# A two-layer encoder trunk: splits moved to VectorE, two more early column blocks, modulation moved to other stages

## The chip, the cores and the metric

The kernel runs on one core of a Trainium2 chip, as one launch. The metric is the device time of a launch in microseconds; a profiled execution gives the trace. The engines are TensorE (PE; its weight loads are listed apart as PEld), VectorE (DVE), ScalarE (ACT), GpSimd (POOL) and SyncE (SP), whose queue issues nearly all DMAs. Each engine works through its own list of instructions in order and waits on semaphores.

## The reference, cut to what matters

x is 1024 tokens by 1024 channels. Each of two layers does the following:

```python
mod = silu(c) @ w_mod[l] + b_mod[l]            # six rows of 1024: sh_a sc_a gt_a sh_f sc_f gt_f
h = rms_norm(x, g_attn[l]) * (1 + sc_a) + sh_a
qa, ka, va, qb, kb, vb, qc, kc, vc = split_cols(h @ w_in[l], IN_SPLITS)
...                                            # three head groups A, B, C and their norms
x = x + gt_a * (y @ w_o[l])                    # output projection
h = rms_norm(x, g_ffn[l]) * (1 + sc_f) + sh_f
gate, up = split_cols(h @ w_gu[l], (2816, 2816))
x = x + gt_f * ((silu(gate) * up) @ w_down[l])
```

A final RMS norm closes the trunk. All is float32.

## The kernel before, in words

**Splits.** A matmul operand of full precision is held as two tiles: the high part, rounded by ScalarE (`act.copy`), and the low part, the rest, from a subtraction on a second engine. Three matmuls (`mm3`, line 190) make one product. `split_tile` (148) does this for a 128x1024 weight tile `wst` into `whi` and `wlo`; the subtraction is on GpSimd unless `eng` says otherwise. `split_to` (198) does it for 128x512 tiles. Weight tiles share the tag `whl` with eight buffers, the raw tiles the tag `wst` with two.

**Order in a layer.** Projection of group C, then V (8 blocks, 830) and the remaining A/B columns (12 half blocks, 981 to 992), then attention, the output projection (1475 to 1620), gate/up (1622 to 1829) and down. On engines that `pin` names, the order is that of the program; elsewhere it may be changed when the program is built.

**Output projection.** The 1024 tokens are worked off in two halves. In the first, `o_rows` (1500) takes a row block of w_o for six column blocks at once and two further columns follow (1532, 1548); in the second, a loop over eight columns (1596) follows. `w_next` (1481) keeps up to four split weight tiles ahead: row blocks 7, 0 and 1 are split by VectorE, the eleven others by GpSimd. `residual` (1494) adds the result to x, `square_sum` (400) sums the squares of x over channels into `ssq`, and `rstd_rows` (463) yields twice: after the statistics (`rstd_cols`, tile `ps_st`) and after the spread over partitions (`spread`, tile `ps_r`). `h_norm` and `h_shift_split` make the first token half's blocks h11 and h21 here.

**Gate/up.** It multiplies 2x2 blocks by seven products (`PRODUCTS`, 206): operands of h are 11, 21, t2, t1, t3, 22, t4. Column block q runs over 22 values, gate and up in turn. `gu_product` (1662) runs one product of four k, 12 matmuls, and drains it. Products 11, t2, t3 and t4 of a block accumulate in one PSUM bank "a", products t1 and 22 in "c", product 21 in "b". PSUM has eight banks (tag `mm`, bufs=8). Products 11 and 21 need only the first token half of h and single columns of weights, so those of the first EARLY=5 column blocks run first (1788 to 1803), on weights from `first_cols` (1745), while the second half of h is still made: `t2_part`, `t3_part` and `t4_part` (1755 to 1781) norm x, form sums and split them; four of each. The other five products of those blocks follow in the main loop (1808), where `a_parts` (221) forms and splits the weight sums, alternating VectorE and GpSimd by `turn`. `Ahead.fill(n)` makes them up to n ahead.

**Modulation.** Ten groups of 1024 columns (`todo`, 310) are still open when layer 0 starts. One step multiplies 128 rows of w_mod by their element of silu(c) and adds into the tile `acc` (VectorE, with a load of 512 KB); after eight steps a finish sums over partitions with four matmuls (`ps_mod`) and VectorE work. `mod_next` (350) does at most one step per call and finishes on the next; it is called in the V loop (977), once per half block of A/B (987), and in layer 0 in the output projection (1505, 1598). `mod_stream` (364) does the same in halves of 512 columns inside layer 0's gate/up (1783, called at 1822 from q=2 on).

Of the kernel before, what the change touches and what calls it, by code (L numbers as in the profile page):

```python
# [10 lines left out]
F32 = mybir.dt.float32  # L11
# [8 lines left out]
P = 128  # L20
D = 1024
S = 1024
KC = D // P
H = 512
FF = 2816
# [60 lines left out]
def trunk(ctx: ExitStack, tc, A, C, out):  # L86
# [90 lines left out]
    C_COLS = [(1408, 1920)]  # L177
    V_COLS = [(512, 768), (1280, 1408), (1920, 2048)]

    def w_cols(w, c0):  # L180

        return split_w(
            lambda v: [(v, w[:, c0 : c0 + P].rearrange("(k p) n -> p k n", p=P))], KC
        )

    def w_rows(w, r0, hl=None, eng=None):
# [34 lines left out]
    def a_parts(raws, sums, m, first, turn):  # L221

        def part(src):
            t = wp.tile([P, 2, 4, P], F32R, name="wpt", tag="whl", bufs=8)
            dst = t[:, 0, :m], t[:, 1, :m]
            turn[0] += 1
            split_to(dst, src, (dve, pool)[turn[0] % 2])
            return dst  # L230

        r1, r2 = raws
        a11, a21 = r1[:, :m, :P], r1[:, :m, P:]
        a12, a22 = r2[:, :m, :P], r2[:, :m, P:]
# [12 lines left out]
        yield part(a22)  # L247
# [63 lines left out]
    going = {"step": 0}  # L311

    def mod_parts(c, shared):
        pl, tag, bufs, width = shared
        acc = going["acc"]
        hi = pl.tile([P, width], F32R, name="acch", tag=tag, bufs=bufs)
        lo = pl.tile([P, width], F32R, name="accl", tag=tag, bufs=bufs)
        dve.tensor_copy(hi, acc[:, c])
        dve.tensor_tensor(out=lo, in0=acc[:, c], in1=f32(hi), op=ALU.subtract)
        going["parts"] = c.start, hi, lo, shared  # L320
        going["wait"] = width < 1024

    def mod_flush(psp):

# [22 lines left out]
        mod_finish(*todo.pop(0), sums)  # L347
        going["step"] = 0

    def mod_next(psp, shared, l):  # L350


        if psp is not None:
            mod_flush(psp)
        if not todo or todo[0][0] > l or going["step"] == KC:
            return
        if going["step"] == 0:
            going["acc"] = cp.tile([P, 1024], F32, name="acc", tag="acc")
        mod_step(*todo[0], going["step"], going["acc"], shared)
        going["step"] += 1  # L360
        if going["step"] == KC:
            mod_parts(slice(0, shared[3]), shared)
# [329 lines left out]
    for l in range(2):  # L692
# [281 lines left out]
        for t in range(8):  # L974
            v_split(t, early[t] if t < len(early) else v_proj(t))
            if t > 1:
                mod_next(psl, (ab, "zt", 4, 1024), l)

        wab = split_tile(wst.pop(0), KC)
        store = None  # L980
        for oc in range(NE, 8):
            w = wab
            for half in range(2):
                if half == 0 and oc < 7:
                    wab = split_tile(wst.pop(0), KC)
                ps = ab_proj(w, half)
                mod_next(psl, (ab, "zt", 4, 1024), l)
                if store:
                    store()
                if half == 0 and oc < 6:  # L990
                    wst.append(w_ab(l, oc + 2))
                store = ab_split(oc, half, ps, ab)
# [488 lines left out]
        def w_next():  # L1481

            while due and len(wq) < 4:
                kind, i = due.pop(0)
                eng = dve if kind == "row" and i in (7, 0, 1) else pool
                if kind == "row":
                    wq.append(w_rows(w_o, i * P, eng=eng))
                else:
                    wq.append(w_cols(w_o, i * P))
            return wq.pop(0)  # L1490

        pss = [psl.tile([P, 512], F32, name="ps_o", tag="mm") for _ in range(NK)]
# [7 lines left out]
        def o_rows(ki, hi, lo):  # L1500
            wh, wl = w_next()
            for n in range(NK):
                ns = slice(n * P, (n + 1) * P)
                mm3(pss[n], wh[:, ns], wl[:, ns], hi, lo, ki == 0, ki == 7)
            for _ in range(0 if l else (1, 1, 1, 1, 1, 0, 0, 0)[ki]):
                mod_next(None, (mp, "wm", 2, 1024), 0)

        for ki in range(5):
            o_rows(ki, yq[:, ki, 0:H], yq[:, ki, H:S])
# [85 lines left out]
        ssq = square_sum(ntp, xt, 0, 1)  # L1595
        for i, n in enumerate((6, 7, 0, 1, 2, 3, 4, 5)):
            w = wc[i] if i < KC - NK else w_next()
            if l == 0:
                mod_next(psl, (mp, "wm", 2, 1024), 0)
            if i < 4:  # L1600
                spill(0, range(2 * i, 2 * i + 2))
            ps = psl.tile([P, 512], F32, name="ps_o", tag="mm")
# [8 lines left out]
            if i == 3:  # L1611
                rows = next(norm)
                for k in range(KC):
                    h_norm(k, 0, rows)
                    h_shift_split(("11", "21")[k % 2], k // 2, xt[:, k, 0:H], shift(k))
        mod_flush(psl)
        ssq = square_sum(ntp, xt, 1, 1)
        spill(1)
        close(mp_cm)
# [4 lines left out]
        ff_cm, ffp = open_pool("ffn", side="left")  # L1624
        hb_cm, hbp = open_pool("hb", side="right")
        h_tiles(hbp, ("t2", "t1", "t4", "22", "t3"))
        turn = [0]

        def x_tile(n, shape, name):
            return xp.tile(shape, F32, name=name, tag=f"x{n}")  # L1630
# [31 lines left out]
        def gu_product(q, p, a):  # L1662
# [5 lines left out]
            lo, hi = slice(0, H), slice(H, S)  # L1668

            def take(key, out=None):  # L1670
                if out is None:
                    tag, bufs = ("u4", 1) if (q, num) == (4, 1) else ("u", 4)
                    out = ffp.tile([P, H], F32, name="u", tag=tag, bufs=bufs)
                t[key] = out
                act.copy(out, ps)
# [68 lines left out]

        def first_cols(c0):
            rows = w_gu[:, c0 : c0 + P].rearrange("(k h p) n -> h p k n", h=2, p=P)
            return split_w(lambda v: [(v[:, 4 * i : 4 * i + 4], rows[i]) for i in range(2)], KC)

        dsh = ffp.tile([P, 4], F32, name="dsh")
        for i in range(4):  # L1750
            sub(dsh[:, i : i + 1], shift(2 * i + 1), shift(2 * i))
        EARLY = 5
        early = [first_cols(q % 2 * FF + q // 2 * 2 * P) for q in range(4)]

        def t2_part(i, rows):

# [9 lines left out]
            sub(b11, b12, b11)  # L1766
            shifted_sub(t2, b22, shift(k + 1), b11)
            h_split("t2", i, t2, dve)
            h_split("t1", i, b11, pool)
            return b12, b21, b22, t2  # L1770

        def t3_part(i, b12, b21, b22, t2):

            shifted_sub(b12, b22, dsh[:, i : i + 1], b12)
            h_split("t3", i, b12, pool)

        def t4_part(i, b12, b21, b22, t2):

            h_shift_split("22", i, b22, shift(2 * i + 1))
            shifted_sub(b21, b21, shift(2 * i + 1), t2)  # L1780
            h_split("t4", i, b21, pool)

        mods_due = mod_stream(psl, (ntp, "sq", 2, H), (1, 4))
        bs = []
        rows = None
        norm = rstd_rows(ssq, ntp, psl)
# [1 line left out]
        for q in range(EARLY):  # L1788
            for i in range(2):
                a = [w[:, 4 * i : 4 * i + 4] for w in early[q]]  # L1790
                gu_product(q, PRODUCTS[i], a)
                if q == 0:
                    rows = next(norm)
            if q == 0:
                early.append(first_cols(2 * 2 * P))
                raw0 = gu_raw(0)
            if q < 4:
                bs.append(t2_part(q, rows))
            if q == 0:
                t3_part(0, *bs[0])  # L1800
                t4_part(0, *bs[0])
            if q == 3:
                ahead.fill(5)
        for part in (t3_part, t4_part):
            for q in range(1, 4):
# [2 lines left out]
        for q in range(NF):  # L1808
# [9 lines left out]
            for i, p in enumerate(PRODUCTS[2 if q < EARLY else 0 :]):  # L1818
                gu_product(q, p, ahead.get())
                ahead.fill()  # L1820
                g_step()
                if q > 1:
                    next(mods_due, None)
        for _ in mods_due:
            pass
# [313 lines left out]
```

## Time and profile before

| | |
|---|---|
| median of 3 runs | 2606.36 us |
| the runs | 2606.36, 2611.0, 2601.78 us |
| the profiled execution | 2610.04 us |
| its span, first to last instruction | 2608.3 us |
| mean granted TensorE clock | 0.975 |
| HBM read, written | 267.31 MB, 87.85 MB |

The profile lists for each engine its busy time, for groups of equal instructions (output tile <- input tiles) count, busy time and mean, and the idle time before them with the instruction that ended it (after "<-"). A window is a stretch of the span with the busy time of each engine; a timeline lists instructions in order with their start and duration. Nearly all instructions carry line 49, that of the helper which records them, so tiles are the way to find them. Durations of neighbouring instructions overlap a little.

### The profile page before, as it was taken

The page shows a single profiled execution, that of the slowest core. Times are in us where ns is not written, and L with a number is a line of the kernel's source. Part 1 is how long each engine was busy: PE and PEld are TensorE (multiplying, and loading weights), DVE is VectorE, ACT ScalarE, POOL GpSimd, SP SyncE. Part 2 cuts the span into 40 slices and gives each one's busy share as a digit, 9 for nine tenths or more (in the row PEclk, how much of TensorE's full clock was granted, in tenths as well). Part 3 has the DMA queues.
Part 4 walks back from the last instruction along what each step waited for, and adds up shares of the span by engine and source line. Part 5 has one row for each costly group of instructions (what it writes and reads, how often), then busy time and mean ns, then how long its engine had stood idle before and what let it go on. Part 6 is the DMA issues. An engine that isn't in the chain of part 4 may idle for free.

```text
span 2608.3 us, 34639 instructions
## 1 busy us (share of the span) xinstructions
PE 2455.3 (94%) x12071; PEld 2024.9 (78%) x12071; DVE 1836.1 (70%) x2916; ACT 1241.4 (48%) x2335; POOL 974.2 (37%) x881
## 2 busy tenths in 40 slices
PE   5899999988899999989998999998999999998998
PEld 4677899776677777878886779987877888886887
DVE  6845999987978786377657449998587455445865
ACT  5421888943433333334543128898444333333443
POOL 5641445643643444300044224465446434430001
PEclk9999999998999999999999999999999999998999
DMA  8467205165244543296432760151624233228643
GB/s 265 141 186 232 61 18 151 39 219 176 89 146 162 169 157 123 88 290 199 135 97 68 212 191 25 25 156 43 202 65 145 93 106 105 93 97 248 203 140 108
DMA packets 291166, 356.48 MB, mean 137 GB/s; under 512 B 33080, under 2 KB 207376, under 8 KB 290992
## 3 DMA queue, kind: packets, MB, share of 16 engines
q1 hardware_dynamic: 290688, 354.14, 44.1%
q8 instruction: 95, 1.56, 0.2%
q14 instruction: 79, 0.65, 0.1%
q0 software_dynamic: 304, 0.14, 0.0%
HBM read 267.31 MB, written 87.85 MB: 136 GB/s over the span
## 4 chain that ended last, share of the span: by engine, by line
PE 47%; DVE 7%; issue 4%; DMA 3%; ACT 2%; POOL 2%; SPq 1%; POOLq 0%; DVEq 0%; ACTq 0%
PE ps_w L49 19%; PE ps_d L49 12%; PE ps_o L49 3%; PE pv L49 3%; PE ps_ab L49 2%; PE T L49 2%; PE ps_v L49 2%; PE sC L49 2%; DMA wmt<-in_w_mod_dram 1%; SPq L49 1%; DVE wpt L49 1%; DVE acc L49 1%; DVE xb L49 1%; DVE sg L49 1%; DVE ws L49 1%
## 5 line engine op out<-in xcount | busy, mean ns | idle before, releaser
L49 PE MATMUL ps_d<-wpt 128*128 128x512 f32 x1848 | 432.1, 395 | 17.7 <-ACT wpt L49 17.3
L49 PEld LDWEIGHTS ps_d<-wpt 128*128 128x128 f32 x1848 | 350.1, 190 | 95.2 <-ACT wpt L49 18.4
L49 POOL TENSOR_SCALAR pr<-pr,rs 128x1024 f32<-128x1024 f32 (+4 forms) x256 | 208.1, 815 | 223.1 <-DVE rs L49 208.9
L49 POOL TENSOR_TENSOR wlo<-wst,whi 128x1024 fp32r<-128x1024 f32 x58 | 148.4, 2561 | 263.9 <-ACT whi L49 251.5
L49 PE MATMUL pv<-pt,vs 128*128 128x256 f32 x1216 | 200.7, 296 | 11.0 <-DVE y L49 4.9
L49 DVE TENSOR_TENSOR pt<-T,pt 128x512 fp32r<-128x512 f32 x304 | 199.7, 681 | 10.2 <-ACT pt L49 8.7
L49 PE MATMUL T<-identr,pr 128*128 128x128 f32 x1320 | 191.9, 274 | 5.5 <-POOL pr L49 2.6
L49 POOL TENSOR_TENSOR wpt<-ws,wpt 128x512 fp32r<-128x512 f32 x88 | 122.9, 1399 | 191.8 <-ACT wpt L49 136.1
L49 ACT CAST wpt<-w 128x512 fp32r<-128x512 f32 x154 | 95.6, 621 | 200.2 <-PE ps_d L49 184.8
L49 ACT CAST pt<-T 128x512 fp32r<-128x512 f32 x304 | 170.0, 586 | 40.3 <-PE T L49 38.4
L49 ACT COPY u<-ps_w 128x512 f32<-128x512 f32 x132 | 77.4, 586 | 219.4 <-PE ps_w L49 219.4
L49 POOL TENSOR_TENSOR sg<-sg,u 128x512 f32<-128x512 f32 x88 | 128.0, 1455 | 142.7 <-DVE u L49 70.8
L49 PEld LDWEIGHTS pv<-pt,vs 128*128 128x128 f32 x1216 | 160.6, 189 | 25.4 <-DVE y L49 12.5
L49 PEld LDWEIGHTS T<-identr,pr 128*128 128x128 f32 x1320 | 156.6, 141 | 27.5 <-POOL pr L49 4.7
L49 DVE TENSOR_TENSOR wpt<-w,wpt 128x512 fp32r<-128x512 f32 x154 | 108.0, 701 | 90.6 <-ACT wpt L49 90.6
L49 DVE SCALAR_TENSOR_TENSOR acc<-wmt,condT,acc 128x512 f32<-128x512 f32 (+1 forms) x99 | 125.1, 1273 | 46.9 <-DMA wmt<-in_w_mod_dram 46.4
L49 ACT CAST wpt<-ws 128x512 fp32r<-128x512 f32 x176 | 108.1, 622 | 70.8 <-PE ps_w L49 31.3
L49 DVE TENSOR_TENSOR wpt<-ws,wpt 128x512 fp32r<-128x512 f32 x88 | 83.5, 949 | 79.0 <-ACT wpt L49 78.9
L49 PE MATMUL ps_w<-ht3h,wpt 128*128 128x512 f32 x352 | 114.0, 406 | 15.0 <-ACT sg L49 15.0
L49 DVE TENSOR_TENSOR ws<-wr 128x512 f32<-128x512 f32 x88 | 87.4, 995 | 56.9 <-POOL wpt L49 53.4
L49 ACT CAST whi<-wst 128x1024 fp32r<-128x1024 f32 x74 | 77.2, 1049 | 104.2 <-PE ps_o L49 46.7
L49 DVE TENSOR_REDUCE rs<-sC 128x1 f32<-128x1024 f32 x96 | 116.9, 1220 | 10.2 <-PE sC L49 9.9
(258 smaller groups left out, 6279.4 us busy)
## 6 DMA issues: line engine op xcount, KB each, us to landing
wr<-in_w_gu_dram SPq DMA_DIRECT2D x92, 512.0 KB, 4.2
gpd<-sg SPq DMA_DIRECT2D x154, 256.0 KB, 4.5
graw<-gpd SPq DMA_DIRECT2D x76, 512.0 KB, 3.6
w<-in_w_down_dram SPq DMA_DIRECT2D x110, 256.0 KB, 5.3
wmt<-in_w_mod_dram SPq DMA_DIRECT2D x47, 512.0 KB, 5.2
qk<-qkd SPq DMA_DIRECT2D x44, 512.0 KB, 7.3
wmt<-in_w_mod_dram SPq DMA_DIRECT2D x66, 256.0 KB, 3.6
qkd<-qko SPq DMA_DIRECT2D x64, 256.0 KB, 3.8
```

What stands on the lines that cost most here:

```text
L49: ins = op(*args, **kwargs)
```

## The change

1. `w_cols` takes an engine, and `w_next` gives VectorE for all rows and columns of w_o. `first_cols` gives VectorE. `h_split` of t1, t3 and t4 goes to VectorE (t2 was there). `turn` starts at -10, which sends the first ten weight parts of gate/up to VectorE.
2. EARLY is 7. The weights of early block q+4 are fetched behind block q, and the raw tiles of the main loop after them. The statistics of the second half come behind both products of block 0, the spread behind block 1, the parts t2 of i behind block i+1, and five weight parts are made ahead behind block 5. The outputs of product 11 of blocks 5 and 6 lie in a tile that shares the buffer of `acc`.
3. No modulation step runs in the output projection. Beside V and A/B the calls are one per V block, as before, and two per A/B half block; they go up to group (0, 4) in layer 0 and through (1, 5) in layer 1. The stream in layer 0's gate/up starts at q=7 and takes (0, 5) to (1, 2). A finish always waits one call more.

```diff
-    def w_cols(w, c0):
+    def w_cols(w, c0, eng=None):
...
-            split_to(dst, src, (dve, pool)[turn[0] % 2])
+            split_to(dst, src, (dve, pool)[max(turn[0], 0) % 2])
...
-        going["wait"] = width < 1024
+        going["wait"] = True
...
-    def mod_next(psp, shared, l):
+    def mod_next(psp, shared, until):
...
-        if not todo or todo[0][0] > l or going["step"] == KC:
+        if not todo or todo[0] >= until or going["step"] == KC:
...
             if t > 1:
-                mod_next(psl, (ab, "zt", 4, 1024), l)
+                mod_next(psl, (ab, "zt", 4, 1024), ((0, 5), (2, 0))[l])
...
                 ps = ab_proj(w, half)
-                mod_next(psl, (ab, "zt", 4, 1024), l)
+                for _ in range(2):
+                    mod_next(psl, (ab, "zt", 4, 1024), ((0, 5), (2, 0))[l])
...
-                eng = dve if kind == "row" and i in (7, 0, 1) else pool
                 if kind == "row":
-                    wq.append(w_rows(w_o, i * P, eng=eng))
+                    wq.append(w_rows(w_o, i * P, eng=dve))
                 else:
-                    wq.append(w_cols(w_o, i * P))
+                    wq.append(w_cols(w_o, i * P, eng=dve))
...
-            for _ in range(0 if l else (1, 1, 1, 1, 1, 0, 0, 0)[ki]):
-                mod_next(None, (mp, "wm", 2, 1024), 0)
...
-            if l == 0:
-                mod_next(psl, (mp, "wm", 2, 1024), 0)
...
-        mod_flush(psl)
...
-        turn = [0]
+        turn = [-10]
...
             def take(key, out=None):
+                if num == 1 and 5 <= q < EARLY:
+                    out = spare[:, (q - 5) * H : (q - 4) * H]
...
-            return split_w(lambda v: [(v[:, 4 * i : 4 * i + 4], rows[i]) for i in range(2)], KC)
+            return split_w(
+                lambda v: [(v[:, 4 * i : 4 * i + 4], rows[i]) for i in range(2)], KC, eng=dve
+            )
...
-        EARLY = 5
+        EARLY = 7
         early = [first_cols(q % 2 * FF + q // 2 * 2 * P) for q in range(4)]
+        raw0 = None
+        spare = cp.tile([P, 1024], F32, name="spare", tag="acc")
...
-            h_split("t1", i, b11, pool)
+            h_split("t1", i, b11, dve)
...
-            h_split("t3", i, b12, pool)
+            h_split("t3", i, b12, dve)
...
-            h_split("t4", i, b21, pool)
+            h_split("t4", i, b21, dve)
...
-        mods_due = mod_stream(psl, (ntp, "sq", 2, H), (1, 4))
+        mods_due = mod_stream(psl, (ntp, "sq", 2, H), (1, 3))
...
                 gu_product(q, PRODUCTS[i], a)
-                if q == 0:
-                    rows = next(norm)
+            if q + 4 < EARLY:
+                early.append(first_cols((q + 4) % 2 * FF + (q + 4) // 2 * 2 * P))
+            elif raw0 is None:
+                raw0 = gu_raw(0)
             if q == 0:
-                early.append(first_cols(2 * 2 * P))
-                raw0 = gu_raw(0)
-            if q < 4:
-                bs.append(t2_part(q, rows))
-            if q == 0:
+                next(norm)
+            if q == 1:
+                rows = next(norm)
+            if 1 <= q < 5:
+                bs.append(t2_part(q - 1, rows))
+            if q == 1:
                 t3_part(0, *bs[0])
                 t4_part(0, *bs[0])
-            if q == 3:
+            if q == EARLY - 2:
                 ahead.fill(5)
...
-                if q > 1:
+                if q >= EARLY:
                     next(mods_due, None)
```

More of the change, by code (lines that the diff above doesn't have):

```diff
@@ L178, in trunk @@
     V_COLS = [(512, 768), (1280, 1408), (1920, 2048)]
-    def w_cols(w, c0):
+    def w_cols(w, c0, eng=None):
         return split_w(
-            lambda v: [(v, w[:, c0 : c0 + P].rearrange("(k p) n -> p k n", p=P))], KC
+            lambda v: [(v, w[:, c0 : c0 + P].rearrange("(k p) n -> p k n", p=P))], KC,
+            eng=eng,
         )
```

## The prediction, made before the changed kernel ran

> **What bounds the kernel now.** I read the page first, then the windows of equal stages in the two layers, then TensorE's timeline for the idle times inside them, and last VectorE's and GpSimd's lists at those places.
>
> ```profile
> span 2608.3 us, 34639 instructions
> PE 2455.3 (94%) x12071; PEld 2024.9 (78%) x12071; DVE 1836.1 (70%) x2916; ACT 1241.4 (48%) x2335; POOL 974.2 (37%) x881
> ...
> 1978.43 378.27 PE ps_w L49 x1620
> ```
>
> TensorE is the bound. In the chain of waits, gate/up of the second layer runs 1620 matmuls in 378.27 us without a break, 0.2335 us each. One early block (two products of 12 matmuls) is therefore 24 x 0.2335 = 5.6 us, and a product 2.8. A change can win only TensorE's idle time and the slow matmuls behind it. Both layers do the same work, but only the first carries modulation beside it, so windows of the same stage show where time goes (output projection; start of gate/up until the first t3 product; rest of gate/up; then the same for layer 1; columns: length, busy time and count of PE, PEld, DVE, ACT, POOL, granted clock, DMA share, GB/s):
>
> ```profile
> 528.50:629.70 101.20, 94.84 (x425) 77.57 (x424) 80.52 (x89) 39.43 (x52) 40.56 (x17) 0.98 0.69 226
> 629.70:688.20 58.50, 39.46 (x158) 30.86 (x156) 50.59 (x58) 26.06 (x42) 29.82 (x18) 0.84 0.19 59
> 688.20:1108.20 420.00, 408.26 (x1724) 326.26 (x1724) 301.70 (x357) 149.46 (x267) 183.52 (x125) 0.99 0.44 142
> 1817.00:1909.80 92.80, 92.80 (x421) 76.78 (x420) 60.97 (x73) 41.50 (x55) 41.48 (x18) 0.99 0.56 184
> 1909.80:1962.20 52.40, 40.33 (x157) 31.65 (x156) 44.62 (x51) 23.89 (x39) 27.43 (x17) 0.88 0.14 42
> 1962.20:2362.00 399.80, 399.71 (x1704) 321.15 (x1704) 206.23 (x245) 150.48 (x266) 171.97 (x125) 0.99 0.32 106
> ```
>
> The start of gate/up (rows two and five) holds 12 to 19 us of idle TensorE at a clock of 0.84 to 0.88; the output projection of layer 0 is 8.4 us longer than that of layer 1, and the rest of its gate/up 20.2 us longer. TensorE's own rows name the waits:
>
> ```profile
> 542.52 1.49 PE L49 MATMUL ps_r<-identr,rstd 128*128 128x128 f32 x8 [3.90 <-DVE rstd L49]
> 587.79 0.73 PE L49 MATMUL ps_mod<-acch,onesr 128*128 128x512 f32 x2 [1.48 <-DVE acch L49]
> 591.12 0.74 PE L49 MATMUL ps_mod<-accl,onesr 128*128 128x512 f32 x2 [0.98 <-DVE accl L49]
> 641.56 1.87 PE L49 MATMUL ps_st<-onesr,ssq 128*128 128x1 f32 x8 [8.67 <-DVE ssq L49]
> 688.26 1.22 PE L49 MATMUL ps_w<-ht3h,wpt 128*128 128x512 f32 x2 [8.09 <-ACT sg L49]
> ...
> 1915.59 1.87 PE L49 MATMUL ps_st<-onesr,ssq 128*128 128x1 f32 x8 [2.77 <-DVE ssq L49]
> 1946.87 0.50 PE L49 MATMUL ps_w<-ht2h,wpt 128*128 128x512 f32 x1 [1.64 <-ACT wpt L49]
> 1948.49 0.50 PE L49 MATMUL ps_w<-ht2h,wpt 128*128 128x512 f32 x1 [1.13 <-POOL wpt L49]
> 1950.09 1.05 PE L49 MATMUL ps_w<-ht2h,wpt 128*128 128x512 f32 x2
> 1962.22 1.22 PE L49 MATMUL ps_w<-ht3h,wpt 128*128 128x512 f32 x2 [6.55 <-ACT sg L49]
> ```
>
> All of them end at VectorE or at what follows it. At 1962.22 the releaser ACT is only the messenger: its copy of the product's bank stands in its queue behind a cast that waits for VectorE.
>
> ```profile
> 1961.06 0.62 ACT L49 CAST ht4h<-xb 128x512 fp32r<-128x512 f32 x1 [2.72 <-DVE xb L49]
> 1961.59 0.58 ACT L49 COPY sg<-ps_w 128x512 f32<-128x512 f32 x1
> ```
>
> Why VectorE is late shows when its rows are laid beside GpSimd's (first three lines VectorE, fourth GpSimd, then VectorE's groups from 1923 to 1964):
>
> ```profile
> 1930.06 0.68 DVE L49 TENSOR_TENSOR ht2l<-t,ht2h 128x512 fp32r<-128x512 f32 x1
> 1930.66 1.78 DVE L49 SCALAR_TENSOR_TENSOR xb<-xb,mod,t 128x512 f32<-128x512 f32 x1
> 1932.36 0.67 DVE L49 TENSOR_TENSOR u<-u,ps_w 128x512 f32<-128x512 f32 x1
> 1930.20 1.69 POOL L49 TENSOR_TENSOR ht3l<-xb,ht3h 128x512 fp32r<-128x512 f32 x1 [1.28 <-ACT ht3h L49]
> ...
> L49 DVE SCALAR_TENSOR_TENSOR xb<-xb,mod,t 128x512 f32<-128x512 f32 x4 | 6.0, 1508 | 0.0
> L49 DVE SCALAR_TENSOR_TENSOR h22l<-xb,mod,h22h 128x512 fp32r<-128x512 f32 x4 | 6.0, 1498 | 0.0
> L49 DVE SCALAR_TENSOR_TENSOR xb<-xb,gsc,ps_r 128x512 f32<-128x512 f32 x8 | 5.7, 736 | 0.0
> L49 DVE SCALAR_TENSOR_TENSOR xb<-xb,dsh 128x512 f32<-128x512 f32 x4 | 5.5, 1368 | 0.0
> L49 DVE TENSOR_TENSOR xb<-xb 128x512 f32<-128x512 f32 x4 | 5.2, 1298 | 0.0
> ```
>
> The VectorE operation that starts while GpSimd is in its split takes 1.78 us and ends 0.55 us after it; operations that read PSUM (the ps_r and ps_w rows) keep 0.74 and 0.67. Against 0.74 (0.68 for the plain subtraction) the four slow groups lose 4 x (0.77 + 0.76 + 0.63 + 0.62) = 11.1 us. With smaller excesses in groups not shown, I take 14 us of some 41.
>
> The Trainium skill, page "SBUF — State Buffer", section "SBUF: two separate sides", says that VectorE operations with two SBUF inputs and GpSimd operations exclude each other through one shared port pair for a whole instruction. These rows agree with it, including the untouched PSUM readers. By it the 14 us vanish with GpSimd's splits; if the slowness were VectorE's own, t3 would begin some 13 us later in each layer and the time would be 26 us above my sum.
>
> **The change part by part.** *Splits moved to VectorE (w_next, first_cols, h_split, first ten weight parts).*
>
> ```profile
> L49 POOL TENSOR_TENSOR wlo<-wst,whi 128x1024 fp32r<-128x1024 f32 x58 | 148.4, 2561 | 263.9 <-ACT whi L49 251.5
> ...
> 1818.80 1.23 DVE L49 TENSOR_TENSOR wlo<-wst,whi 128x1024 fp32r<-128x1024 f32 x1 [0.38 <-ACT whi L49]
> ```
>
> A 1024-wide split is 2.56 us on GpSimd and 1.23 on VectorE; a 512-wide one 0.68. Eleven splits per output projection cost VectorE 11 x 1.23 = 13.5 us; it is busy 61.0 of 92.8 us in layer 1 and, without the thirteen modulation steps, no more than that in layer 0, so they fit at no cost. Whatever queues behind such a split (residuals, ssq, h_norm) waits with it for its cast.
>
> The work on h's second half, as VectorE's busy time in a window, its last operation, and GpSimd's last split:
>
> ```profile
> 1923.10:1962.20 39.10, 39.10 (x42) 0.92 0.09 27
> 1962.62 1.77 DVE L49 SCALAR_TENSOR_TENSOR xb<-xb,mod,t 128x512 f32<-128x512 f32 x1
> 1965.49 1.74 POOL L49 TENSOR_TENSOR ht4l<-xb,ht4h 128x512 fp32r<-128x512 f32 x1
> ```
>
> From the first h_norm (1923.1) VectorE has no idle time until 1964.4, 41.3 us. Less 14, plus 12 splits of h (12 x 0.6, the distance of the 0.68 us rows above), two first_cols splits (2.5; the third falls earlier), three weight parts and two additions of early products (5 x 0.6): 41.3 - 14 + 7.2 + 2.5 + 3.0 = 40.0 us, with the low halves of h among it, whose last GpSimd now ends at 1967.2.
>
> *Seven early blocks.* The statistics move behind the second product, so ssq gets 2.8 us more cover: all of the 2.77 us wait of layer 1. In layer 0 the 8.67 us should go too, for its ssq additions stand behind modulation steps that are removed. The first h_norm then comes 5.6 + 1.9 (statistics) + 5.6 + 0.5 (spread) = 13.6 us after the start, against 13.3 now, but TensorE then still has five blocks (28 us) in place of four. The t3 product can begin 7 x 5.6 + 2.4 + 5.6 = 47.2 us after the start, or about 1957.1 on the old clock; VectorE has its last h at 1923.4 + 40.0 = 1963.4, and TensorE wants it, in the fourth k of t4, at 1964.8. That is tight. Remaining waits per layer: nothing at the low end, today's 6.55 + 1.64 + 1.13 = 9.3 us at the high end; I take 3.0, near the low end, because the work balances. So 50.2 us in place of 52.4. The rest of gate/up loses two blocks (11.2) and, with a shorter stall, about 1 us of slow matmuls (at 1950.09 two last 1.05 us): 399.8 - 12.2 = 387.6. **Layer 1: 452.2 - 437.8 = 14.4 us won.** The additional loads are two columns of 512 KB while DMA is at 42 GB/s: hidden.
>
> The Trainium skill, page "TensorE: Matmul & The Clock Gate", Part 1, puts the return to half rate after an idle window of about 3.4 us. Here the matmuls were already slow behind waits of 1.64 and 1.13 us; by the rule my 3.0 us would leave no slow matmuls and the sum would be 2 us lower in all.
>
> *Modulation out of layer 0's output projection.* Thirteen steps and their 512 KB loads leave VectorE and the SP queue, with one finish. The three waits at 542, 588 and 591 are 6.4 us, plus slow matmuls; layer 1 shows the stage without them: 101.2 - 92.8 = **8.4 us won** (5 to 9). The gate/up stream has four groups in place of four and a rest that ends a fifth: of 20.2 us it keeps four fifths, 16.2. So layer 0's gate/up goes from 58.5 + 420.0 = 478.5 to 437.8 + 16.2 = 454.0: **24.5 us won**.
>
> *More modulation beside the V and A/B projections.* Six more steps in layer 0, eight in layer 1:
>
> ```profile
> 209.27 0.71 PE L49 MATMUL ps_mod<-acch,onesr 128*128 128x512 f32 x2 [1.28 <-DVE acch L49]
> 195.00:262.00 67.00, 65.72 (x283) 52.96 (x282) 35.25 (x40) 10.78 (x16) 12.61 (x4) 1.00 0.77 232
> 1450.00:1460.00 10.00, 10.00 (x45) 8.10 (x44) 1.38 (x2) 0.89 (x2) 4.74 (x10) 1.00 0.91 319
> ```
>
> VectorE has 30 us to spare for 8 x 1.3. DMA goes from 232 to (15.5 + 3.1 MB) / 67 us = 279 GB/s, below the 319 seen nearby. The mod loads stand in SP's queue ahead of the qko stores and the next w_ab load, and that load is two blocks (22 us) ahead. Each layer gains one finish: four matmuls (1 us) and up to 1.3 of waiting. I take 1.5 per layer, **3.0 us lost** (0 to 5). That a finish now waits one call more gives VectorE time and costs nothing.
>
> Sum: 14.4 + 8.4 + 24.5 - 3.0 = 44.3 us. The profiled execution took 2610.04 (its span 2608.3), 3.7 above the median of the runs; 2606.4 - 44.3 = **2562 us**.
>
> **The rivals.** *PSUM runs out.* Bank "a" of every early block stays open until its last product, so seven of eight banks are held when block seven runs, and each second product waits for VectorE's addition of the one before.
>
> ```profile
> 1944.33 0.68 DVE L49 TENSOR_TENSOR u<-u,ps_w 128x512 f32<-128x512 f32 x1
> 1953.56 0.67 DVE L49 TENSOR_TENSOR u<-u,ps_w 128x512 f32<-128x512 f32 x1
> ```
>
> The second of these is the fifth block's, which ended at 1946.87 - 1.64 = 1945.2: it is 8 us late, the one before, 5.6 us earlier, some 5. If that lateness stays, TensorE waits as much as today: 9.3 - 3.0 + 2 (slow matmuls) = 8.3 us per layer, 2562 + 17 = 2579. For it: VectorE's balance has no slack. Against: the lateness is about the 14 us that go.
>
> *The DMA queue becomes the bound in A/B.* At two loads per half block TensorE's 5.6 us meet 1.05 MB of modulation, 0.52 of stores and 0.26 of weights; at today's 232 GB/s that is 7.9 us, 2.3 too long in some six halves per layer before the buffers' wait thins it out: 28 us, 2590. Against: 319 GB/s was reached.
>
> *Slower: VectorE inherits GpSimd's waits.* GpSimd stood 251.5 us waiting for whi casts, 4.3 for each of 58 splits. If 18 splits per layer make VectorE stand 3 us each, and everything behind them is late by as much, that is 108 us against 44 won: 2670. It decides from 1.2 us per split on. Against: the casts are paced by TensorE, as are the residuals behind them, and the split that VectorE already has there waits 0.38 us.
>
> **How the numbers follow.** Forecast 0.58 (its own range 2551 to 2574, from the bounds above), PSUM 0.18, DMA 0.10, the last two together with no net change 0.04, slower 0.10. A measurement of this kernel tells about 0.3% (8 us) from no change. Faster 0.86, same 0.04, slower 0.10. The range takes in the forecast's low end, PSUM and DMA: 2547 to 2592.
>
> **What would show it.** Right: VectorE's xb rows all at 0.74 from the start of gate/up; no ssq wait; t3 beginning 47 to 51 us after the first ps_w in both layers; the output projection near 93 us in layer 0; A/B still without idle TensorE. Wrong: ps_w waiting for DVE u (banks), a wait for wlo in the A/B projection (DMA), wlo rows on VectorE with idle time of 1.2 us or more and ps_o waiting behind them.

## The result, and the profile after

The changed kernel takes 2571.97 us (median of 4 runs, 2568.89 to 2575.07) against 2604.11 for the kernel before (median of 4, 2601.78 to 2611.0): ratio 0.9872, 95% interval 0.9847 to 0.9897. It is 32 us faster; 44 were forecast. The profiled executions differ by 35.0 us of span. The page's head:

```profile
span 2573.3 us, 34615 instructions
PE 2447.9 (95%) x12071; PEld 2023.2 (79%) x12071; DVE 1835.1 (71%) x2979; ACT 1240.3 (48%) x2331; POOL 830.9 (32%) x811
```

TensorE has the same 12071 matmuls and is busy 7.4 us less (fewer matmuls at a low clock); the rest, 27.6 us, is idle time that is gone. GpSimd has 70 instructions and 143 us of work less. VectorE has 63 instructions more and is busy for no longer: its operations became shorter.

To see where the 35.0 us come from, the span is cut at the first matmul of each stage. This table is worked out from the starts of TensorE's instructions (us). The prediction's windows were cut by eye and differ from these stages by up to 2 us.

| stage | before | after | difference | forecast |
|---|---|---|---|---|
| V and A/B projections, layer 0 | 168.7 | 178.8 | +10.1 | +1.5 |
| output projection, layer 0 | 101.5 | 91.7 | -9.8 | -8.4 |
| gate/up, layer 0, up to the first t3 product | 58.3 | 49.0 | -9.3 | -8.3 |
| the rest of it | 421.5 | 399.6 | -21.9 | -16.2 |
| V and A/B projections, layer 1 | 169.0 | 178.4 | +9.4 | +1.5 |
| output projection, layer 1 | 93.0 | 92.7 | -0.3 | 0 |
| gate/up, layer 1, up to the first t3 product | 52.4 | 49.0 | -3.4 | -2.2 |
| the rest of it | 401.8 | 388.8 | -13.0 | -12.2 |
| all other stages | 1142.1 | 1145.3 | +3.2 | 0 |

The +3.2 of the last row lies mostly ahead of layer 0's projections (+2.1) and in group C of layer 1 (+1.7), where the change does nothing; the experiments' runs differ there among themselves by as much (91.6 to 94.6 us and 44.8 to 47.9). The three gains came, that of layer 0's gate/up bigger than forecast. One term is far off: the V and A/B stages lost 19.5 us, not 3.0. The same windows as in the prediction, with the A/B stages added (length; busy time and count of PE, PEld, DVE, ACT, POOL; granted clock, DMA share, GB/s), first of before, A/B only:

```profile
92.60:261.30 168.70, 161.66 (x723) 129.07 (x723) 95.12 (x124) 43.88 (x84) 67.23 (x51) 0.98 0.66 189
1357.00:1526.00 169.00, 159.99 (x713) 128.43 (x712) 95.13 (x125) 45.47 (x86) 64.28 (x52) 0.97 0.50 146
```

and of after:

```profile
94.70:273.50 178.80, 166.03 (x728) 131.67 (x728) 115.56 (x139) 43.79 (x84) 66.44 (x51) 0.95 0.67 197
542.10:633.90 91.80, 91.80 (x423) 76.08 (x422) 64.17 (x88) 41.54 (x55) 6.58 (x4) 1.00 0.56 186
633.90:682.90 49.00, 46.22 (x206) 37.14 (x204) 42.60 (x68) 25.92 (x42) 1.58 (x1) 1.00 0.23 70
682.90:1082.40 399.50, 392.76 (x1672) 315.01 (x1672) 288.59 (x351) 147.95 (x263) 173.28 (x119) 1.00 0.47 150
1352.20:1530.60 178.40, 164.45 (x717) 131.09 (x716) 116.00 (x142) 41.69 (x81) 58.99 (x45) 0.94 0.59 175
1892.20:1941.20 49.00, 46.24 (x205) 37.16 (x203) 42.70 (x68) 25.90 (x42) 1.57 (x1) 1.00 0.23 70
1941.20:2330.00 388.80, 386.93 (x1656) 313.00 (x1656) 204.81 (x250) 148.57 (x263) 162.96 (x119) 1.00 0.34 110
```

At the start of gate/up the clock is 1.00 in place of 0.84 and 0.88, and GpSimd has one instruction in place of 18 and 17. In A/B of layer 0 TensorE is idle for 178.8 - 166.0 = 12.8 us against 168.7 - 161.7 = 7.0 before, 5.7 more, and busy for 4.4 more, at a lower clock (0.95): together the 10.1.

**Start of gate/up.** VectorE's list in layer 1 of after (third column: what the instruction is) shows how the forecast's mechanism turned out. First h_norm, two rows from the middle, the last rows beside GpSimd's first work, the last h:

```profile
1905.12 0.74 DVE L49 SCALAR_TENSOR_TENSOR xb<-xb,gsc,ps_r 128x512 f32<-128x512 f32 x1
...
1911.36 0.75 DVE L49 SCALAR_TENSOR_TENSOR h22l<-xb,mod,h22h 128x512 fp32r<-128x512 f32 x1
...
1912.63 0.75 DVE L49 SCALAR_TENSOR_TENSOR xb<-xb,mod,t 128x512 f32<-128x512 f32 x1
...
1934.83 2.07 DVE L49 SCALAR_TENSOR_TENSOR xb<-xb,dsh 128x512 f32<-128x512 f32 x3
...
1939.95 1.75 DVE L49 SCALAR_TENSOR_TENSOR h22l<-xb,mod,h22h 128x512 fp32r<-128x512 f32 x1
...
1942.28 1.77 DVE L49 TENSOR_TENSOR ht4l<-xb,ht4h 128x512 fp32r<-128x512 f32 x1
...
1946.66 0.69 DVE L49 TENSOR_TENSOR ht4l<-xb,ht4h 128x512 fp32r<-128x512 f32 x1
```

GpSimd's list at that place:

```profile
1939.57 1.57 POOL L49 TENSOR_TENSOR sg<-sg,u 128x512 f32<-128x512 f32 x1 [122.28 <-ACT sg L49]
1941.77 1.73 POOL L49 TENSOR_TENSOR sg<-sg,u 128x512 f32<-128x512 f32 x1 [0.62 <-DVE h22l L49]
```

The operations that averaged 1.3 to 1.5 us before take 0.69 to 0.75 as long as GpSimd is idle, and 1.75 again within half a microsecond of GpSimd's first multiplication. VectorE is done 1946.66 + 0.69 - 1905.12 = 42.2 us after the first h_norm; the forecast was 40.0. One wait is left before t3. The chain of waits still runs through VectorE's list, up to ht4l at 1945.3, and from there through a copy of ScalarE to TensorE's long run of matmuls (start, length, instruction and count):

```profile
1931.22 3.09 DVE wpt L49 x5
1934.31 0.60 DVE spare L49
1934.91 1.99 DVE xb L49 x3
1936.90 1.80 DVE ht3l L49 x3
...
1942.36 1.69 DVE ht4l L49
...
1946.04 376.74 PE ps_w L49 x1620
```

TensorE's own row for the wait before t3, and a matmul behind it:

```profile
1941.22 1.04 PE L49 MATMUL ps_w<-ht3h,wpt 128*128 128x512 f32 x2 [2.78 <-ACT sg L49]
1942.05 0.63 PE L49 MATMUL ps_w<-ht3l,wpt 128*128 128x512 f32 x1
```

**V and A/B.** TensorE's and VectorE's lists of after, where the A/B half blocks begin, name the wait. First TensorE (the last two rows are of layer 1):

```profile
211.47 1.19 PE L49 MATMUL ps_mod<-acch,onesr 128*128 128x512 f32 x2 [6.95 <-DVE acch L49]
212.71 1.22 PE L49 MATMUL ps_mod<-accl,onesr 128*128 128x512 f32 x2
213.72 0.63 PE L49 MATMUL ps_ab<-hh,whi 128*128 128x512 f32 x1
...
1467.39 1.19 PE L49 MATMUL ps_mod<-acch,onesr 128*128 128x512 f32 x2 [4.81 <-DVE acch L49]
1470.59 1.22 PE L49 MATMUL ps_mod<-accl,onesr 128*128 128x512 f32 x2 [2.00 <-DVE accl L49]
```

Then VectorE in layer 0, from the last V split to the cast that the finish needs:

```profile
194.03 0.69 DVE L49 TENSOR_TENSOR vs<-ps_v,vs 128x512 fp32r<-128x512 f32 x1 [4.90 <-ACT vs L49]
194.64 0.84 DVE L49 TENSOR_SCALAR acc<-wmt,condT 128x1024 f32<-128x1024 f32 x1
...
205.84 2.59 DVE L49 SCALAR_TENSOR_TENSOR acc<-wmt,condT,acc 128x1024 f32<-128x1024 f32 x2
208.54 2.78 DVE L49 CAST acch<-acc 128x1024 fp32r<-128x1024 f32 x1
```

All eight steps of the group stand behind the last V split in VectorE's list and end at 208.5. It is the order of the list that holds them back, not their loads: the first three loads have landed by 187.8. TensorE meets the finish's matmul behind the second A/B half block. In before it met it behind the third:

```profile
209.27 0.71 PE L49 MATMUL ps_mod<-acch,onesr 128*128 128x512 f32 x2 [1.28 <-DVE acch L49]
```

One half block is 5.6 us, and 1.28 + 5.6 = 6.9: the wait that is there. In layer 1 the wait was 1.26, and the two rows of after add up to 6.8.

### The profile page after: what moved, and what is told of

Same layout as the page of the kernel before. It is cut to its first block, busy times and chain, and to the rows that moved or that the text cites. A ratio compares the mean times of both kernels' runs of the same rounds, so it can differ in the third digit from the quotient of the medians.

```text
span 2573.3 us, 34615 instructions
## 1 busy us (share of the span) xinstructions
PE 2447.9 (95%) x12071; PEld 2023.2 (79%) x12071; DVE 1835.1 (71%) x2979; ACT 1240.3 (48%) x2331; POOL 830.9 (32%) x811
## 4 chain that ended last, share of the span: by engine, by line
PE 50%; DVE 6%; issue 4%; DMA 3%; ACT 2%; POOL 1%; SPq 1%; POOLq 0%; DVEq 0%; ACTq 0%
PE ps_w L49 21%; PE ps_d L49 13%; PE ps_o L49 3%; PE pv L49 3%; PE ps_ab L49 3%; PE T L49 2%; PE ps_v L49 2%; PE sC L49 1%; DMA wmt<-in_w_mod_dram 1%; SPq L49 1%; DVE acc L49 1%; DVE ws L49 1%; DVE sg L49 1%; PE ps_st L49 1%; PE sA L49 1%
## 5 line engine op out<-in xcount | busy, mean ns | idle before, releaser
L49 POOL TENSOR_TENSOR sg<-sg,u 128x512 f32<-128x512 f32 x86 | 122.8, 1428 | 385.3 <-ACT sg L49 244.6
L49 PE MATMUL pv<-pt,vs 128*128 128x256 f32 x1216 | 201.1, 297 | 11.4 <-DVE y L49 4.9
L49 DVE TENSOR_TENSOR pt<-T,pt 128x512 fp32r<-128x512 f32 x304 | 199.6, 681 | 12.3 <-ACT pt L49 10.8
L49 POOL TENSOR_TENSOR wpt<-ws,wpt 128x512 fp32r<-128x512 f32 x80 | 112.2, 1404 | 182.7 <-ACT wpt L49 130.9
L49 DVE TENSOR_REDUCE rs<-sC 128x1 f32<-128x1024 f32 x96 | 117.0, 1220 | 10.2 <-PE sC L49 10.1
L49 DVE TENSOR_TENSOR wpt<-graw,wpt 128x512 fp32r<-128x512 f32 x154 | 108.4, 704 | 15.7 <-ACT wpt L49 15.6
```

Of the source, the lines that this page charges most:

```text
L49: ins = op(*args, **kwargs)
```

## The experiments

Theory A: the 19.5 us of A/B are the finish's place in TensorE's list; rival, the doubled modulation loads. Theory B: the gain at the start of gate/up comes from splits that GpSimd no longer does beside VectorE; rival, the two more blocks alone bring it. All times are medians; ratios are against runs of the kernel before made alongside. The kernel before measured 2604.11, 2606.84, 2605.91 and 2603.57 us in the four batches of runs, so a difference of up to 3 us between kernels of different batches tells nothing.

### One call per half block in the first A/B column

```diff
-                for _ in range(2):
+                for _ in range(1 if oc == NE else 2):
```

> The changed kernel, but with one modulation call instead of two in each of the first two A/B half blocks (28 calls remain, as many as the three groups need). Theory 1, place in the list: the two ps_mod waits of the changed kernel (6.95 us in layer 0, 4.97 and 2.4 in layer 1) come from the first finish standing one half block (5.6 us) too early in TensorE's list, while VectorE's eight steps begin only behind the last V split. Then the waits shrink to under 2.5 us per layer, the stretch from the first A/B block to attention falls from 178.8 and 178.4 us to 170 to 173, and the time is 10 to 17 us below the changed kernel, near 2558. Rival, DMA: the loads are what is late; the same loads then arrive as late, the stretch stays at 175 or more, and the time is within 5 us of the changed kernel.

Measured: 2555.07 us (2553.98 to 2557.02), ratio 0.98, interval 0.9786 to 0.9815. The A/B stages take 170.5 and 172.0 us. TensorE's list in layer 0:

```profile
208.54 0.70 PE L49 MATMUL ps_mod<-acch,onesr 128*128 128x512 f32 x2 [1.30 <-DVE acch L49]
209.07 0.39 PE L49 MATMUL ps_ab<-hh,whi 128*128 128x512 f32 x1
```

The window of the stage:

```profile
91.90:262.40 170.50, 162.92 (x727) 129.81 (x726) 111.29 (x135) 45.32 (x86) 65.68 (x51) 0.98 0.70 208
```

The same loads go through at 208 GB/s in place of 197, and the wait is back at 1.30 us. Theory A holds; the loads are not the bound. This version is 17 us faster than the changed kernel.

### The finish still one half block later

```diff
-                for _ in range(2):
+                for _ in range({0: 1, 1: 1, 2: 1, 3: 3}.get(2 * (oc - NE) + half, 2)):
```

> As the run with one call in the first two A/B half blocks, but one call in the first three and three in the fourth, so the first finish stands one half block later still. Place in the list: the ps_mod wait of 1.3 us goes, A/B is 169.5 to 171 us in both layers, time 2551 to 2554. DMA: three loads in one half block make the next steps late and a later finish waits: 2555 or more.

Measured: 2557.28 us (2554.09 to 2561.26), ratio 0.9813, interval 0.9799 to 0.9828. No matmul of a finish waits any more, and the stages take 169.6 and 169.9 us. That is 3 us less than in the version above, yet the time is not lower: the spans are 2552.3 and 2552.2, and other stages gave the 3 us back by amounts of 0.5 to 2 us. No gain can be claimed.

### The modulation part alone, on the kernel before

Part 3 of the change, without parts 1 and 2 (the stream in gate/up starts at q=2 as before):

```diff
...
-                mod_next(psl, (ab, "zt", 4, 1024), l)
+                for _ in range(2):
+                    mod_next(psl, (ab, "zt", 4, 1024), ((0, 5), (2, 0))[l])
...
-            for _ in range(0 if l else (1, 1, 1, 1, 1, 0, 0, 0)[ki]):
-                mod_next(None, (mp, "wm", 2, 1024), 0)
...
-        mods_due = mod_stream(psl, (ntp, "sq", 2, H), (1, 4))
+        mods_due = mod_stream(psl, (ntp, "sq", 2, H), (1, 3))
```

> The kernel before with part 3 of the change alone (modulation out of the output projection, two calls per A/B half block, one call more before a finish). Theory: the A/B stretch is as long as in the changed kernel in both layers (178 against 169: 10 us lost each), layer 0's output projection wins 7 to 10 us, the start of its gate/up wins some 6 of the 8.67 us ssq wait, the rest of its gate/up 4 to 6: no net change, 2596 to 2608. Rival, the loss in A/B needs the splits on VectorE: A/B stays near 170 and the time falls to 2585.

Measured: 2607.78 us (2602.06 to 2615.18), ratio 1.0001, interval 0.9991 to 1.0011. Layer by layer: A/B +8.6 and +10.4, output projection of layer 0 -8.7, start of its gate/up -6.1, the rest of it -7.3. By itself this part moves some 20 us from one place to another.

### The splits alone, on the kernel before

Part 1 of the change, with five early blocks and the modulation where it was:

```diff
...
-        turn = [0]
+        turn = [-10]
...
-            h_split("t1", i, b11, pool)
+            h_split("t1", i, b11, dve)
...
```

> The kernel before with part 1 alone (splits of w_o, of first_cols, of h and the first ten weight parts on VectorE; five early blocks, modulation as before). Theory, shared port: VectorE's own operations fall to 0.74 us, which pays for the splits it takes over (14 us against 13), so the t3 product begins 50 to 53 us after the start of gate/up in layer 1 (52.3 before): time 2590 to 2606, a gain of a few us, most of it the end of the short waits. Rival, VectorE as the bound without cover: all splits on one engine make t3 begin later than before, 56 us or more per layer, and the time is 2610 or more.

Measured: 2580.28 us (2578.7 to 2586.28), ratio 0.99, interval 0.9886 to 0.9915. It gains more than was expected: t3 of layer 1 begins 43.7 us after the first ps_w (52.4 before), and layer 0's output projection takes 96.2 us, though the modulation is still in it. Of the 31.4 us by which its span is shorter, 17.8 lie at the start of gate/up in the two layers and 6.6 in the output projections. Why the splits alone do better than was expected was not followed further. TensorE, with two blocks less than in the changed kernel, still waits in layer 1:

```profile
1895.78 1.05 PE L49 MATMUL ps_st<-onesr,ssq 128*128 128x1 f32 x8 [2.03 <-DVE ssq L49]
1923.49 0.49 PE L49 MATMUL ps_w<-ht2h,wpt 128*128 128x512 f32 x1 [1.00 <-ACT wpt L49]
1934.51 1.22 PE L49 MATMUL ps_w<-ht3h,wpt 128*128 128x512 f32 x2 [4.48 <-ACT sg L49]
```

### Five early blocks instead of seven

```diff
-        EARLY = 7
+        EARLY = 5
...
-                if num == 1 and 5 <= q < EARLY:
-                    out = spare[:, (q - 5) * H : (q - 4) * H]
...
-        spare = cp.tile([P, 1024], F32, name="spare", tag="acc")
```

> The changed kernel with five early blocks instead of seven (parts 1 and 3, and the later place of the statistics). Theory: in gate/up the two additional blocks only give cover; splits on VectorE alone took 442.8 us for the whole of layer 1's gate/up, against 437.8 in the changed kernel, and here the first h_norm comes one product later: 443 to 447 in layer 1, waits of 5 us and more before t2 and t3, and a time 10 to 18 us above the changed kernel, 2582 to 2590. Rival, the blocks do nothing once the splits are on VectorE: within 5 us of the changed kernel.

Measured: 2588.08 us (2585.3 to 2591.31), ratio 0.9931, interval 0.9916 to 0.9946. Layer 1's gate/up takes 30.5 us to t2, 14.8 to t3 and 400.5 for the rest, 445.8 in all (437.8 with seven); layer 0's takes 454.4 (448.6 with seven). Two blocks of cover are worth 8.0 us in layer 1 and 5.8 in layer 0.

### The splits back on the old engines, the rest of the change kept

```diff
+                eng = dve if kind == "row" and i in (7, 0, 1) else pool
...
-                    wq.append(w_rows(w_o, i * P, eng=dve))
+                    wq.append(w_rows(w_o, i * P, eng=eng))
...
-        turn = [-10]
+        turn = [0]
...
-            h_split("t1", i, b11, dve)
+            h_split("t1", i, b11, pool)
...
```

> The changed kernel with all splits on the engines they had before (parts 2 and 3 alone). Theory, shared port: VectorE's two-source operations stretch to 1.3 to 1.8 us again, h is ready some 57 us after the start of gate/up, t3 begins at 52 to 56 us instead of 49, and the time is 6 to 18 us above the changed kernel, 2578 to 2590. Rival, the two additional blocks alone are the gain and the engine of the splits does not matter: t3 begins at 47 to 50 us and the time is within 4 us of the changed kernel.

Measured: 2585.2 us (2584.2 to 2588.9), ratio 0.992, interval 0.9903 to 0.9936; t3 begins 57.5 and 59.1 us after the first ps_w. TensorE's waits at the start of layer 1's gate/up, then the operations of VectorE behind them:

```profile
1937.58 0.79 PE L49 MATMUL ps_w<-h21h,whi 128*128 128x512 f32 x1 [5.14 <-DVE spare L49]
1948.38 0.86 PE L49 MATMUL ps_w<-ht1h,wpt 128*128 128x512 f32 x2 [2.96 <-DVE spare L49]
```

```profile
1936.85 0.68 DVE L49 TENSOR_TENSOR spare<-spare,ps_w 128x512 f32<-128x512 f32 x1
...
1940.21 1.77 DVE L49 SCALAR_TENSOR_TENSOR xb<-xb,mod,t 128x512 f32<-128x512 f32 x1
```

The added matmuls run out of PSUM: the last early block's product waits for VectorE's addition of the block before. This is the prediction's rival of the banks; it exists, and the moved splits keep it away.

Theory B's rival holds in part. Layer 1's gate/up, which carries no modulation, takes 454.2 us before, 442.8 with the splits alone, 446.2 here with the blocks (and with the modulation moved, which by itself leaves 453.0) and 437.8 with all. There the splits by themselves are worth 11.4 us, this part 8.0, and 3.0 of the sum overlap.

### One set of splits back at a time

Only those of h:

```diff
-            h_split("t1", i, b11, dve)
+            h_split("t1", i, b11, pool)
...
-            h_split("t3", i, b12, dve)
+            h_split("t3", i, b12, pool)
...
-            h_split("t4", i, b21, dve)
+            h_split("t4", i, b21, pool)
```

> The changed kernel with the splits of t1, t3 and t4 of h back on GpSimd, all other splits on VectorE. Theory, shared port at h: these twelve splits per layer stretch VectorE's sums again, its additions of the early products come late, and block seven waits for its PSUM bank (5.14 us with all splits back): gate/up of layer 1 lasts 442 to 446 us instead of 437.8 and the time is 8 to 16 us above the changed kernel, 2580 to 2588. Rival: the splits of w_o, of first_cols and of the weight parts made the difference: within 4 us of the changed kernel, no bank wait.

Measured: 2577.67 us (2576.38 to 2578.78), ratio 0.9889, interval 0.9873 to 0.9906. Only 5.7 us are lost, less than expected. The wait for a bank is back, but small: TensorE waits 1.33 us for `spare` in layer 1, at 1937.52.

Only those of the early columns and of the first ten weight parts of gate/up:

```diff
-        turn = [-10]
+        turn = [0]
...
-                lambda v: [(v[:, 4 * i : 4 * i + 4], rows[i]) for i in range(2)], KC, eng=dve
+                lambda v: [(v[:, 4 * i : 4 * i + 4], rows[i]) for i in range(2)], KC
```

> The changed kernel with the splits of first_cols and of the first gate/up weight parts back on GpSimd, the splits of h and of w_o on VectorE. Undoing all the moved splits cost 13 us (2585.2), undoing those of h alone 5.7 (2577.7). If what is missing lies with these splits, the time is 2576 to 2582, the t3 product of the second layer begins 52 to 56 us after the first ps_w in place of 49.0, and VectorE again has rows of 1.7 us at the start of gate/up. Rival: the two sets of splits only hurt together, or what is missing lies with w_o: then within 3 us of the changed kernel, 2569 to 2575, and t3 at 49 to 51 us.

Measured: 2579.32 us (2575.32 to 2581.55), ratio 0.9899, interval 0.9879 to 0.9918. t3 begins 55.1 and 56.7 us after the first ps_w. VectorE's groups at the start of layer 1's gate/up, two of them again with a mean above 1.5 us:

```profile
L49 DVE SCALAR_TENSOR_TENSOR xb<-xb,mod,t 128x512 f32<-128x512 f32 x4 | 6.1, 1531 | 0.0
...
L49 DVE TENSOR_TENSOR wpt<-ws,wpt 128x512 fp32r<-128x512 f32 x2 | 3.1, 1534 | 0.1
```

TensorE's wait there is again one for a bank:

```profile
1943.00 1.16 PE L49 MATMUL ps_w<-ht1h,wpt 128*128 128x512 f32 x2 [2.76 <-DVE spare L49]
```

Only those of w_o:

```diff
+                eng = dve if kind == "row" and i in (7, 0, 1) else pool
...
-                    wq.append(w_rows(w_o, i * P, eng=dve))
+                    wq.append(w_rows(w_o, i * P, eng=eng))
...
-                    wq.append(w_cols(w_o, i * P, eng=dve))
+                    wq.append(w_cols(w_o, i * P))
```

> The changed kernel with the splits of w_o back as they were: row blocks 7, 0 and 1 on VectorE, the eleven others on GpSimd. The prediction costed their move at nothing, since VectorE has idle time in the output projection. If so, the time stays within 3 us of the changed kernel (2569 to 2575) and both output projections stay at 91.7 to 93 us. Rival: GpSimd's splits delay the residuals and squares at the end of the stage, and with them the first h_norm: then TensorE waits for ssq at the start of gate/up, t3 begins 51 to 55 us after the first ps_w, and the time is 2576 to 2582.

Measured: 2574.02 us (2571.21 to 2576.41), ratio 0.9883, interval 0.9862 to 0.9904; both output projections take 93.0 us and t3 begins after 49.0. In the medians the three sets cost 5.7, 7.4 and 2.1 us more than the changed kernel, 15 together; all at once cost 13. But in these runs' traces the A/B stages, which the edits don't touch, are 1 to 3 us shorter than in the changed kernel. The gate/up stages alone tell more (one trace each): both layers together take 886.4 us in the changed kernel, 892.5 with h's splits back, 898.2 with those of the early columns and weight parts, 902.9 with all and 885.3 with those of w_o. So the early columns and weight parts carry about twice as much as h's splits, 11.8 us against 6.1, and w_o's move is worth nothing that can be told.

### The copy before t3 on VectorE

The one wait left before t3 ends at a copy of ScalarE. On the version with no finish waiting, that copy was given to VectorE:

```diff
-                act.copy(out, ps)
+                if q == 0 and num == 6:
+                    dve.tensor_copy(out, ps)
+                else:
+                    act.copy(out, ps)
```

> The same, and the copy of the first t2 product out of its bank is made by VectorE instead of ScalarE. In the changed kernel the t3 product of block 0 waits 2.9 us for that copy (gap of 3.17 us between two matmuls in both layers), which stands behind a table load, a Silu and a cast in ScalarE's list. If that is the cause, the gap falls below 1 us and the time by another 3 to 6 us, 2546 to 2550. If instead h is what is late (VectorE), the gap stays or moves to the 22 product, and nothing is won.

Measured: 2568.46 us (2566.64 to 2575.34), ratio 0.986, interval 0.9845 to 0.9876: 11 us slower than without it. TensorE's wait in layer 0:

```profile
677.72 1.22 PE L49 MATMUL ps_w<-h22h,wpt 128*128 128x512 f32 x2 [7.59 <-ACT sg L49]
```

The built order changed: product 22 now runs ahead of t3 and waits for a ScalarE copy again. That copy, at 677.09, itself waited 3.37 us until VectorE's ht4l was done, by the profile: what the expectation describes for the case that h is late. But as the order changed too, the edit doesn't say what the wait would be without ScalarE; what sets the last 3 us before t3 stays open.

## Why the prediction was right, and where it was wrong

**Right in direction and mechanism.** GpSimd's splits held VectorE up, and without them its rows are at 0.69 to 0.75. This is shown from both sides: they turn slow again where GpSimd's multiplications begin, and the early columns' and weight parts' splits put back alone bring back rows of 1.5 us and the time with them. The case that the slowness is VectorE's own falls with that. The Trainium skill, page "SBUF — State Buffer", section "SBUF: two separate sides", has a VectorE operation with two SBUF inputs and a GpSimd operation that reads SBUF lock each other out of a port pair for a whole instruction; the traces agree (0.69 to 0.75 us alone, 1.75 beside GpSimd).

**Layer 1's gate/up: right in its terms.** 437.8 us were forecast and 437.8 measured (49.0 to t3 where 50.2 was forecast, 388.8 for the rest where 387.6 was), but that the two are equal is luck: the forecast's window of before ended at 2362.0, 2.1 us ahead of the first matmul of the next stage, which the measured 437.8 run up to. Like for like 16.4 us were won, from 454.2, where 14.4 were forecast. The 3.0 us of remaining waits were 2.78, and slow matmuls stand behind them (0.63 us at 1942.05). The prediction's other case, no slow matmuls and 2 us less in all, did not come. The ssq wait is gone, as forecast. The forecast's measure of VectorE, 40.0 us, was 42.2: the two slow rows at the end, 1.0 us too long each, are paid to GpSimd's gate multiplications, which the sum had left out.

**Output projection of layer 0: right**, 9.8 us won where 8.4 was forecast. The splits fit at no cost, as the run with w_o's splits put back shows, and the modulation part alone wins 8.7.

**Layer 0's gate/up: the gain was too small.** 31.2 us measured, 24.5 forecast. The start agrees (49.0 against 50.2). The term that failed is "it keeps four fifths, 16.2": what the modulation stream costs in the rest of the stage is 399.6 - 388.8 = 10.8 us. Its share of VectorE fell only from 301.7 - 206.2 = 95.5 to 288.6 - 204.8 = 83.8, by an eighth, while its price fell by nearly half. The modulation part alone, on the kernel before, already has 414.2 - 400.8 = 13.4 there in place of 421.5 - 401.8 = 19.7, while the splits alone leave it at 420.0 - 399.1 = 20.9; so the group that was taken out cost more than a fifth. The changed kernel with five early blocks, whose stream starts at q=5, has 409.2 - 400.5 = 8.7, so the late start at q=7 isn't needed for the fall. What sets a group's price stays open.

**A/B: the step that failed.** "I take 1.5 per layer, 3.0 us lost", with "that a finish now waits one call more gives VectorE time and costs nothing". 19.5 us were lost. The step priced the work (steps, loads, matmuls) but not the place of the first finish. Steps 1 to 6 of the first group come in the V loop at one call per block. Before, steps 7 and 8 and the finish took one half block each, so that the finish stood behind the third. After, two calls per half block put both steps behind the first, and the wait of one call and the finish behind the second. So the finish came one half block earlier, in spite of the call it waits, while VectorE's eight steps still stood behind the last V split in its list. The row of 1.28 us that was there before, plus the 5.6 us of a half block, would have given it. To 5.7 us of additional wait come the slow matmuls behind it: with the 4 to 5 matmuls more that the stage has, one every 0.23 us, about 1 of the 4.4 us of additional busy time is work, the rest is clock. The Trainium skill, page "TensorE: Matmul & The Clock Gate", Part 1, names an idle window of about 3.4 us for this. These two waits agree with it: behind that of 6.95 us the matmuls take 0.63 us, behind that of 1.30 in the first experiment 0.39. Slow matmuls behind 2.78 us, as above, don't.

**The rivals.** The DMA queue in A/B falls: the same loads in the same stage with the finish moved cost 1.8 and 3.0 us, against the 1.5 that was forecast for them. The banks don't bind in the changed kernel: the early additions of `spare` run at 1928.1 and 1934.2 and nothing waits for them. They do as soon as VectorE is slowed (5.14 and 2.96 us). The slower rival falls: VectorE's 52 splits of 128x1024 waited 24.2 us for casts, 0.47 each, against the 1.2 from which it decides.

```profile
L49 DVE TENSOR_TENSOR wlo<-wst,whi 128x1024 fp32r<-128x1024 f32 x52 | 72.3, 1394 | 28.8 <-ACT whi L49 24.2 <-PE ps_r L49 3.7
```

**The forecast of 2562** thus held errors of opposite sign: it had A/B 16.5 us too cheap, and its gains were too small by 8 us in layer 0's gate/up and output projection and by 2 in layer 1's gate/up. That the time came out only 10 us above the forecast is in part luck. With A/B mended by the first experiment, the kernel measures 2555.

## What to carry to other kernels

A small matmul that waits for another engine's chain must be placed by when that chain ends, not by how many calls lie between: count the blocks of TensorE's list that stand ahead of it before and after an edit, and compare with the time at which the other engine's own list comes to that chain. Work taken off GpSimd pays twice where VectorE is late, once for its own time and once for the VectorE operations beside it, so count both. Blocks added as cover need PSUM banks: look for waits behind the engine that drains them. With GpSimd's splits kept, 8.1 us of such waits stood against two blocks in layer 1, and they still took 8.0 us off its gate/up; with the splits moved there were no such waits.

## What was not expected of the hardware

A cast with one input is held up like an operation with two. The cast of `acc` (128x1024) took 2.78 us in after, where a GpSimd split began 0.11 us ahead of it and ended at 210.77; the cast ended 0.55 us later. GpSimd's row:

```profile
208.43 2.34 POOL L49 TENSOR_TENSOR wlo<-wst,whi 128x1024 fp32r<-128x1024 f32 x1 [13.50 <-ACT whi L49]
```

VectorE's rows in before, where GpSimd's split (204.13 to 207.25) fell on the modulation step ahead of the cast:

```profile
203.71 4.61 DVE L49 SCALAR_TENSOR_TENSOR acc<-wmt,condT,acc 128x1024 f32<-128x1024 f32 x2
208.43 0.69 DVE L49 CAST acch<-acc 128x1024 fp32r<-128x1024 f32 x1
```

Two steps took 4.61 us there against 2.59 in after, and the cast 0.69 against 2.78: the chain pays the same 2 us to GpSimd once, in the one operation or in the other. So the cast's length is not the cause of the longer wait, though it stands right in front of it; the place in TensorE's list is.
